# A fused decoder layer on one core: ten weight-pair sums moved from the up projection into attention, and five pairs by seven products in four chunks

## The chip, the cores and the metric

The kernel runs on one core of one Trainium2 chip. Its time is the device time of one execution, in microseconds (us). The profile is one further execution with the hardware profiler on; its spans and instruction times are those of that execution.

## The reference

One decoder layer on 256 positions of width 2048, all in float32:

```
p = rmsnorm(x) @ w_in                      # q, k, v of 8 heads; latents of 8 more
A = dilated window attention(q, k, v); B = latent attention
x = x + rmsnorm(concat(A, B) @ w_out)
h = rmsnorm(x) * gain
u = square(relu(h @ w_up))                 # w_up: 2048 x 8192
out = x + rmsnorm(u @ w_down)              # w_down: 8192 x 2048
```

## The kernel before

**Precision and tiles.** Each float32 operand is split into a rounded part `hi` and a rest `lo`; a product takes three matmuls (hi hi, hi lo, lo hi), each 128x128 by 128x512. ScalarE makes `hi` (L293, or L297 with a gain folded in), VectorE `lo` (L294, L298). `Weights` streams weight tiles of 128 x 1024 in the order in which they were planned: a load into one of 5 `raw` buffers on the SP queue, then the split into one of 8 `hi`/`lo` buffers. When TensorE's program begins tile i, the splits up to tile i+6 have been issued. Every engine takes its instructions strictly in the order issued. `Flow` writes that order down: a clock advanced by estimated matmul times, and chains (generators) that issue their next piece when the clock reaches it.

**Stages.** Projections and both attentions to about 300 us, the output projection to about 350, the up projection to about 700, the down projection to the end. The two halves of x stand in `xs` from the start; they are used for the first norm (`prelude`, `pre`), then not until `powers` scales them by `pw` during the output projection (L829).

**The up projection.** Eight chunks (j = 0 to 7) of 1024 columns. In chunk 0, 16 tiles of 128 rows (steps "k") go by 12 matmuls each (2 token blocks x 2 halves x 3). In chunks 1 to 7 three pairs of tiles (rows 0 to 5, steps "w" 0, 1, 2) go by seven products instead of eight: 21 matmuls per pair instead of 24. That needs sums of the four quarter blocks of a pair on the weights' side, called t and u, and sums of h on the other side (`left_sums`). The order of a chunk is k6 to k10, w0, k11, k12, w1, k13, w2, k14, k15. For a "w" step POOL loads the two raw tiles into the buffer `ab` (L360; there is one, so the next pair waits until the last split of the earlier one has read it), VectorE makes t and u (L345, L349, L350: "pair sums"), and four tiles are split from SBUF: a quarter (512 wide), b, u and t (1024 wide each). The sums are issued two tiles ahead of the pair's first tile. A "k" tile has the norm's gain folded into its split.

`left_sums(kp)` adds hi and lo of h for one pair, scales by the gain, makes the sums (L963 to L973), and puts the scaled h back in place. The seven products also use four extra accumulators m[1], m[6], m[7], m[5], in the banks of the previous chunk; after the last pair `close` combines them into `c`: a copy on ScalarE (L1005) and four VectorE operations (L1008):

```
scalar.activation(c[0], m[1], AF.Copy)
for out, x, y, op in ((1, m[6], c[0], SUB), (2, m[7], c[1], SUB),
                      (1, m[5], c[1], ADD), (3, c[1], m[7], SUB)):
    tt(out=c[out], in0=x, in1=y, op=op)
```

The next chunk accumulates in those four banks, in the order m[1], m[6], m[7], m[5]. Meanwhile `up_evac` empties the last chunk's four accumulators, one after another: VectorE adds `c` (L909), ScalarE makes `r` (relu, L912), TensorE transposes it (`rt`, L287), ScalarE squares (L924).

Of the kernel before, what the change touches and what calls it, by code (L numbers as in the profile page):

```python
# [92 lines left out]
D_UP, UP_STEP = 1.8, 2.2  # L93


N_SEVEN, SUMS_AHEAD = 3, 2
UP_STEPS = [("k", k) for k in range(6, 11)]
for _i, _n in enumerate(((11, 12), (13,), (14, 15))):
    UP_STEPS += [("w", _i)] + [("k", k) for k in _n]


DOWN_SEVEN = ((7, 11, 13, 17, 19, 23, 25, 29), (4, 7, *range(9, 28, 2)))
# [148 lines left out]
def layer(nc, tc, io):  # L251
# [77 lines left out]
        return io["w_up"][k * P:(k + 1) * P, j * CW:(j + 1) * CW]  # L329

    late = {}

    def seven(load, targets):

        st, tt, H = {}, nc.vector.tensor_tensor, 512

        def sums():
            ab = load()  # L340
            a, b = st["a"], st["b"] = [ab[:, :CW], ab[:, CW:]] if not isinstance(ab, list) else ab
            t, u = st["t"], st["u"] = targets()
            if not isinstance(ab, list):
                two = [x.rearrange("p (k n) -> p k n", n=H) for x in (t, ab)]
                tt(out=two[0], in0=two[1][:, 0:2, :], in1=two[1][:, 1:4:2, :], op=OP.add)  # L345
            else:
                for x, o in ((a, 0), (b, H)):
                    tt(out=t[:, o:o + H], in0=a[:, o:o + H], in1=x[:, H:], op=OP.add)
# [14 lines left out]
    def seven_up(j, kp):  # L363
        def load():
            if j == FF // CW - 1 and kp:
                return [weights.load(up_weight(j, 2 * kp + i), CW, f"raw_w{j}_{kp}{i}") for i in range(2)]
            return load_two(late["ab"], nc.gpsimd if (j, kp) > (1, 0) else nc.sync,
                            io["w_up"][2 * kp * P:(2 * kp + 2) * P, j * CW:(j + 1) * CW])
# [30 lines left out]


    wide_u, after = [], 0
    for j in range(FF // CW):
        wide_u.append([])
        for what, k in [("k", k) for k in range(KD)] if j == 0 else UP_STEPS:
            if what == "k":
                ts = [weights.plan(up_weight(j, k), 1, CW, gcol[:, 8 + k:9 + k])]
            else:
                ts, after = plan_seven(*seven_up(j, k), after)
            wide_u[j].append((what, k, ts))
# [121 lines left out]
    def prelude():  # L531
# [14 lines left out]
        nc.vector.reduce_sum(ss0, ss0h, axis=mybir.AxisListType.X)  # L546
        rstd0.append(rstd_of(ss0, NB, D, "pre"))

    def tables():

        yield D_TAB[0]
        nc.scalar.dma_start(out=pos_i, in_=io["pos"])
        nc.scalar.dma_start(out=cst, in_=io["consts"])
        yield D_TAB[1]
        pos_f = con.tile([P, NB], F32, name="pos_f")
        nc.vector.tensor_copy(pos_f, pos_i)
        ang = pa.tile([P, 2, NB, 96], F32, tag="qkT", bufs=2, name="ang")
# [12 lines left out]
        yield 4.0  # L570
        nc.scalar.activation(trig, ang, AF.Sin)
# [77 lines left out]

    pre = flow.start(prelude())  # L650
    tab = flow.start(tables())
    heads, evacs = [], []
    for half in range(2):
        qkv = {}
# [156 lines left out]
    def powers():  # L811
        po, g_post = late["po"], late["g_post"]
        yield 8.0
        for n in range(4):
            junk = po.tile([P, 512], BF16, tag="junk", bufs=1, name=f"junkg{n}")
            nc.scalar.activation(junk, g_post[:, n * 512:(n + 1) * 512], AF.Square, accum_out=gg4[:, n:n + 1])
            yield 1.5
        nc.vector.reduce_sum(gg, gg4, axis=mybir.AxisListType.X)
        nc.vector.tensor_scalar_add(pws[:, 3, :], ss0, gg)
        r = rstd_of(pws[:, 3, :], NB, D, "pw")  # L820
        yield 2.0
        nc.vector.tensor_single_scalar(out=pw.bitcast(I32), in_=r.bitcast(I32), scalar=0x7F800000, op=OP.bitwise_and)
        nc.vector.tensor_single_scalar(out=pwi.bitcast(I32), in_=pw.bitcast(I32), scalar=0x7F800000, op=OP.bitwise_xor)
        nc.vector.tensor_scalar_mul(pwi, pwi, 0.5)
        for i, (v, c) in enumerate(((pwi, 1.0 / D), (pwi, EPS), (pw, EPS))):
            nc.vector.scalar_tensor_tensor(out=pws[:, i, :], in0=v, scalar=c, in1=v, op0=OP.mult, op1=OP.mult)
        for b in range(NB):
            for c in (slice(0, CW), slice(CW, D)):
                nc.vector.tensor_scalar_mul(xs[b][:, c], xs[b][:, c], pw[:, b:b + 1])  # L829
                yield 1.5  # L830
# [74 lines left out]
    def up_evac(j, b, i, acc, order, more=None):  # L905
# [11 lines left out]
        if j not in uT:  # L917
            if j in (12, 13):
                t2 = late["ab"][:, (j - 12) * CW:(j - 11) * CW]
            else:  # L920
                tag = {"tag": "T", "bufs": 2} if j > 13 else {}
                t2 = late["up"].tile([P, CW], F32, name=f"uT{j}", **tag)
# [35 lines left out]
    def left_sums(kp):  # L958
# [5 lines left out]
        for i in range(2):  # L964
            nc.vector.tensor_scalar_mul(f[:, i * S:(i + 1) * S], f[:, i * S:(i + 1) * S], gcol[:, 8 + k + i:9 + k + i])
        four_sums(q, f)
        st = [late["st"][:, i * 512:(i + 1) * 512] for i in (2 * kp, 2 * kp + 1)]
        yield 3.0
        for t, x in ((hs, f), (st, q)):
            nc.scalar.activation(t[0], x, AF.Copy)  # L970
# [3 lines left out]
        sums.append([[t[:, i * P:(i + 1) * P] for t in st] for i in range(4)])  # L974
        yield 0.5

    def all_sums():
        for kp in range(N_SEVEN - 1):
            yield from left_sums(kp)
        yield 8.0  # L980
        yield from left_sums(N_SEVEN - 1)

    def three(out, a, w, first, last):

# [3 lines left out]
    def seven_products(ts, left, accs, m, first, last):  # L988
# [2 lines left out]
        prods = ((a11, 0, 0, 1), (a12, 1, 0, (0, 0)), (s4, 1, 1, (0, 1)), (s2, 2, 0, 6), (a22, 2, 1, (1, 0)),  # L991
                 (s3, 3, 1, 7), (s1, 3, 0, 5))
        for p, (a, i, half, to) in enumerate(prods):
            w = weights.get(ts[i])
            in_m = isinstance(to, int)
            three(m[to] if in_m else accs[to], a, [w[x][:, half * 512:half * 512 + 512] for x in range(2)],
                  in_m and first, in_m and last)
# [18 lines left out]
    for j in range(FF // CW):  # L1016
# [9 lines left out]
        for t, b in order:  # L1026
            what, k, tiles = steps[t]
            if (j, t, b) == (0, 8, 0):
# [4 lines left out]
                late["st"] = late["up"].tile([P, 3 * CW], F32R, tag="st", bufs=1, name="st")  # L1033
                for n in ("ab", "c"):
                    late[n] = late["up"].tile([P, 2 * CW], F32, name=n)
                flow.start(all_sums())
            if (j, t, b) == (FF // CW - 1, 4, 0):
                weights.limit -= 1
                u_next = split_u(0, 0)
            if j == 1 and what == "w":  # L1040
                flow.until(lambda: len(sums) > k)
            if what == "k":
                w = weights.get(tiles[0])
# [220 lines left out]
```

## Time and profile before

| | us |
|---|---|
| median of 3 runs (1052.40 to 1053.32) | 1052.87 |
| the profiled execution, its own time | 1052.05 |
| its span, first to last instruction | 1050.3 |
| TensorE (PE) busy | 1039.0 |
| VectorE (DVE) busy | 811.0 |
| ScalarE (ACT) busy | 625.4 |
| POOL busy | 61.5 |

The span leaves out 1.75 us of the execution's own time. Rows of a timeline give start, duration, engine, line, operation, output <- inputs, shape and count; a bracket at the end is the idle time before it and what ended it. Rows of the stage table give the stretch, its length, the busy time of PE, PEld, DVE, ACT and POOL, the granted clock (1.00 is full), the DMA engines' share and GB/s. A wait row gives total, count and longest.

### The profile page before, as it was taken

The numbers are of one execution on the slowest core, as the hardware profiler recorded it, in microseconds if no ns is written. First come the engines' busy times: TensorE is split into PE (matmuls) and PEld (weight loads), VectorE is DVE, ScalarE is ACT, GpSimd is POOL, SyncE is SP. The second block draws the span as 40 slices with busy tenths as digits, with TensorE's granted clock in tenths as the row PEclk, the third lists the DMA queues.
The fourth block names the chain that finished last, engine by engine and source line by source line (L and its number), as shares of the span: only waits on it lengthen the run. The fifth ranks groups of instructions, "written<-read, shape, count | busy, mean of one in ns | idle before, by whom it ended". The sixth has DMA issues, their size and how long they took to land.

```text
span 1050.3 us, 13459 instructions
## 1 busy us (share of the span) xinstructions
PE 1039.0 (99%) x4854; PEld 865.9 (82%) x4854; DVE 811.0 (77%) x1080; ACT 625.4 (60%) x834; POOL 61.5 (6%) x116
## 2 busy tenths in 40 slices
PE   9999999999999999999999999999999999999996
PEld 6888899888888788888888888888888888888885
DVE  6676536577557679879888798887899978989995
ACT  6675436565555467666665666666567564766661
POOL 0000000000000000010000000000000001112100
PEclk9999999999999999999999999999999999999999
DMA  8975447454447295646556465469788767788952
GB/s 298 371 230 155 140 127 239 141 166 155 141 170 234 77 344 174 224 143 238 194 189 201 145 234 194 151 227 319 246 276 315 267 223 259 268 300 313 381 186 81
DMA packets 80643, 229.34 MB, mean 218 GB/s; under 512 B 7616, under 2 KB 12224, under 8 KB 80192
## 3 DMA queue, kind: packets, MB, share of 16 engines
q1 hardware_dynamic: 65888, 176.45, 50.3%
q0 software_dynamic: 14112, 51.39, 14.2%
q8 instruction: 38, 0.62, 0.2%
q10 hardware_dynamic: 576, 0.64, 0.2%
q14 instruction: 29, 0.24, 0.1%
HBM read 212.72 MB, written 15.73 MB: 218 GB/s over the span
## 4 chain that ended last, share of the span: by engine, by line
PE 96%; DVE 1%; DMA 1%; issue 1%; ACT 0%; POOL 0%; DVEq 0%; POOLq 0%; ACTq 0%
PE y L283 26%; PE acc_u L283 26%; PE acc_o L283 8%; PE m L283 5%; PE md L283 5%; PE acc_v L283 4%; PE acc_qk L283 4%; PE acc_ckv L283 2%; PE acc_ukv L283 2%; PE acc_q L283 2%; PE acc_cq L283 2%; PE acc_k L283 2%; PE acc_uq L283 2%; PE rt L287 1%; PE sc_b L283 1%
## 5 line engine op out<-in xcount | busy, mean ns | idle before, releaser
L294 DVE TENSOR_TENSOR lo<-raw,hi 128x1024 fp32r<-128x1024 f32 (+3 forms) x213 | 241.7, 1152 | 91.5 <-ACT hi L293 90.7
L293 ACT ACTIVATE hi<-raw 128x1024 fp32r<-128x1024 f32 (+3 forms) x213 | 209.5, 999 | 77.6 <-PE y L283 20.8
L283 PE MATMUL acc_u<-hi,hT_hi 128*128 128x512 f32 x386 | 153.3, 397 | 0.0
L283 PE MATMUL acc_u<-hi,hT_lo 128*128 128x512 f32 x386 | 151.0, 391 | 0.4 <-DVE hT_lo L294 0.4
L283 PE MATMUL acc_u<-lo,hT_hi 128*128 128x512 f32 x386 | 150.7, 391 | 0.0
L283 PE MATMUL y<-hi,uhi 128*128 128x512 f32 x376 | 146.8, 390 | 0.0
L283 PE MATMUL y<-hi,ulo 128*128 128x512 f32 x376 | 146.5, 390 | 0.0
L283 PE MATMUL y<-lo,uhi 128*128 128x512 f32 x376 | 146.5, 390 | 0.0
L298 DVE SCALAR_TENSOR_TENSOR lo<-raw,gcol,hi 128x1024 fp32r<-128x1024 f32 x86 | 107.6, 1280 | 11.2 <-ACT hi L297 11.0
L297 ACT ACTIVATE hi<-raw,gcol 128x1024 fp32r<-128x1024 f32 x86 | 97.8, 1151 | 24.8 <-PE acc_u L283 10.9
L283 PEld LDWEIGHTS acc_u<-hi,hT_lo 128*128 128x128 f32 x386 | 72.5, 188 | 16.1 <-DVE hT_lo L294 0.8
L283 PEld LDWEIGHTS acc_u<-lo,hT_hi 128*128 128x128 f32 x386 | 72.6, 188 | 14.2
L283 PEld LDWEIGHTS acc_u<-hi,hT_hi 128*128 128x128 f32 x386 | 72.6, 188 | 13.9
L283 PEld LDWEIGHTS y<-hi,uhi 128*128 128x128 f32 x376 | 70.6, 188 | 14.6
L283 PEld LDWEIGHTS y<-hi,ulo 128*128 128x128 f32 x376 | 70.6, 188 | 14.6
L283 PEld LDWEIGHTS y<-lo,uhi 128*128 128x128 f32 x376 | 70.6, 188 | 14.5
L283 PE MATMUL acc_o<-hi,mixT_hi 128*128 128x512 f32 x128 | 51.9, 405 | 0.0
L294 DVE TENSOR_TENSOR lo<-st_down,hi 128x1024 fp32r<-128x1024 f32 x40 | 48.1, 1220 | 4.0 <-ACT hi L293 3.8
L283 PE MATMUL acc_o<-hi,mixT_lo 128*128 128x512 f32 x128 | 50.2, 392 | 0.0
L283 PE MATMUL acc_o<-lo,mixT_hi 128*128 128x512 f32 x128 | 50.0, 391 | 0.0
L293 ACT ACTIVATE hi<-ab 128x512 fp32r<-128x512 f32 (+1 forms) x38 | 32.0, 842 | 29.3 <-PE acc_u L283 24.4
L293 ACT ACTIVATE hi<-st_down 128x1024 fp32r<-128x1024 f32 x40 | 42.1, 1053 | 11.1 <-PE y L283 9.5
(322 smaller groups left out, 1986.3 us busy)
## 6 DMA issues: line engine op xcount, KB each, us to landing
raw<-in_w_down SPq DMA_DIRECT2D x88, 512.0 KB, 6.0
raw<-in_w_up SPq DMA_DIRECT2D x86, 512.0 KB, 4.5
raw<-in_w_in SPq DMA_DIRECT2D x55, 512.0 KB, 5.0
ab<-in_w_up POOLq DMA_DIRECT2D x36, 512.0 KB, 5.0
raw<-in_w_out SPq DMA_DIRECT2D x32, 512.0 KB, 4.3
ab_down<-in_w_down POOLq DMA_DIRECT2D x20, 512.0 KB, 6.4
ukeep<-ulo SPq DMA_DIRECT2D x15, 512.0 KB, 7.2
ulo<-ukeep POOLq DMA_DIRECT2D x15, 512.0 KB, 5.4
```

The source lines that it names most:

```text
L283: nc.tensor.matmul(out, a, b, start=start, stop=stop)
L287: nc.tensor.transpose(out, a, ident)
L293: nc.scalar.activation(hi, src, AF.Copy)
L294: nc.vector.tensor_tensor(out=lo, in0=src, in1=hi.bitcast(F32), op=OP.subtract)
L297: nc.scalar.activation(hi, src, AF.Copy, scale=g)
L298: nc.vector.scalar_tensor_tensor(out=lo, in0=src, scalar=g, in1=hi.bitcast(F32), op0=OP.mult, op1=OP.subtract)
```

## The change

For ten pairs of w_up (pairs 0 and 2 of chunk 1, pairs 3 and 4 of chunks 2 to 5) the sums t and u are made during attention. A chain `prepare` uses x's two buffers, which are idle after the first norm: POOL loads the raw pair into one, VectorE makes t and u in the other 16 us of the flow's clock later, POOL writes them to HBM (`sums_kept`); after the tenth, x is loaded again, and `powers` waits for that chain and 8 us more. In the up projection a prepared pair (step "p") comes as four loads on the SP queue through `raw`: the quarter and b from w_up, u and t from `sums_kept`. Chunks 2 to 5 then do five pairs by seven products (0 to 4; k10 to k15 remain), in the order k10 k11 k12 w0 p3 w1 k13 w2 p4 k14 k15. Chunk 1 does pairs 0 and 2 prepared, 1 as before. Chunks 6 and 7 keep three pairs. `left_sums` runs for pairs 3 and 4 in chunk 1; since it leaves h scaled, k6 to k9 of chunks 6 and 7 are split without the gain. The sums of h for pairs 3 and 4 stand in a buffer that chunk 5's output uses afterwards.

```diff
@@ -93,10 +93,24 @@
 D_UP, UP_STEP = 1.8, 2.2
-N_SEVEN, SUMS_AHEAD = 3, 2
-UP_STEPS = [("k", k) for k in range(6, 11)]
-for _i, _n in enumerate(((11, 12), (13,), (14, 15))):
-    UP_STEPS += [("w", _i)] + [("k", k) for k in _n]
+SUMS_AHEAD = 2
+NUP = FF // CW
+def steps_of(text):
+    return [(s[0], int(s[1:])) for s in text.split()]
+UP_STEPS = {0: [("k", k) for k in range(KD)]}
+UP_STEPS[1] = steps_of("k6 k7 k8 k9 k10 p0 k11 k12 w1 k13 p2 k14 k15")
+for _j in range(2, 6):
+    UP_STEPS[_j] = steps_of("k10 k11 k12 w0 p3 w1 k13 w2 p4 k14 k15")
+for _j in range(6, NUP):
+    UP_STEPS[_j] = steps_of("k6 k7 k8 k9 k10 w0 k11 k12 w1 k13 w2 k14 k15")
+SCALED = {1: range(6), **{j: range(10) for j in range(2, NUP)}}
+PREP = [(j, k) for j in UP_STEPS for w, k in UP_STEPS[j] if w == "p"]
+D_PREP = (16.0, 1.5, 1.0, 1.0)
 DOWN_SEVEN = ((7, 11, 13, 17, 19, 23, 25, 29), (4, 7, *range(9, 28, 2)))
@@ -329,6 +343,18 @@
         return io["w_up"][k * P:(k + 1) * P, j * CW:(j + 1) * CW]
     late = {}
+    sums_kept = {jk: dram.tile([P, 2 * CW], F32, name=f"sums{jk[0]}_{jk[1]}") for jk in PREP}
+    def pair_sums(ab, t, u):
+        H, tt = 512, nc.vector.tensor_tensor
+        two = [x.rearrange("p (k n) -> p k n", n=H) for x in (t, ab)]
+        tt(out=two[0], in0=two[1][:, 0:2, :], in1=two[1][:, 1:4:2, :], op=OP.add)
+        yield D_PREP[1]
+        tt(out=u[:, :H], in0=t[:, :H], in1=ab[:, 3 * H:], op=OP.add)
+        yield D_PREP[2]
+        tt(out=u[:, H:], in0=u[:, :H], in1=ab[:, 2 * H:3 * H], op=OP.add)
+        yield D_PREP[3]
     def seven(load, targets):
@@ -399,11 +424,17 @@
     wide_u, after = [], 0
-    for j in range(FF // CW):
+    for j in range(NUP):
         wide_u.append([])
-        for what, k in [("k", k) for k in range(KD)] if j == 0 else UP_STEPS:
+        for what, k in UP_STEPS[j]:
             if what == "k":
-                ts = [weights.plan(up_weight(j, k), 1, CW, gcol[:, 8 + k:9 + k])]
+                g = () if k in SCALED.get(j, ()) else (gcol[:, 8 + k:9 + k],)
+                ts = [weights.plan(up_weight(j, k), 1, CW, *g)]
+            elif what == "p":
+                kept = sums_kept[j, k]
+                ts = [weights.plan(src, 1, n) for src, n in (
+                    (up_weight(j, 2 * k)[:, :512], 512), (up_weight(j, 2 * k + 1), CW),
+                    (kept[:, CW:], CW), (kept[:, :CW], CW))]
             else:
                 ts, after = plan_seven(*seven_up(j, k), after)
             wide_u[j].append((what, k, ts))
@@ -546,6 +577,20 @@
         nc.vector.reduce_sum(ss0, ss0h, axis=mybir.AxisListType.X)
         rstd0.append(rstd_of(ss0, NB, D, "pre"))
+    def prepare():
+        ab, tu = xs
+        while pre in flow.chains:
+            yield 0.5
+        for j, kp in PREP:
+            load_two(ab, nc.gpsimd, io["w_up"][2 * kp * P:(2 * kp + 2) * P, j * CW:(j + 1) * CW])
+            yield D_PREP[0]
+            yield from pair_sums(ab, tu[:, :CW], tu[:, CW:])
+            nc.gpsimd.dma_start(out=sums_kept[j, kp], in_=tu)
+        yield 2.0
+        for b in range(NB):
+            nc.gpsimd.dma_start(out=xs[b], in_=io["x"][b * P:(b + 1) * P, :])
     def tables():
         yield D_TAB[0]
@@ -649,6 +694,7 @@
     pre = flow.start(prelude())
     tab = flow.start(tables())
+    prep = flow.start(prepare())
     heads, evacs = [], []
     for half in range(2):
         qkv = {}
@@ -824,6 +870,9 @@
         nc.vector.tensor_scalar_mul(pwi, pwi, 0.5)
         for i, (v, c) in enumerate(((pwi, 1.0 / D), (pwi, EPS), (pw, EPS))):
             nc.vector.scalar_tensor_tensor(out=pws[:, i, :], in0=v, scalar=c, in1=v, op0=OP.mult, op1=OP.mult)
+        while prep in flow.chains:
+            yield 0.5
+        yield 8.0
         for b in range(NB):
             for c in (slice(0, CW), slice(CW, D)):
                 nc.vector.tensor_scalar_mul(xs[b][:, c], xs[b][:, c], pw[:, b:b + 1])
@@ -964,7 +1017,8 @@
         for i in range(2):
             nc.vector.tensor_scalar_mul(f[:, i * S:(i + 1) * S], f[:, i * S:(i + 1) * S], gcol[:, 8 + k + i:9 + k + i])
         four_sums(q, f)
-        st = [late["st"][:, i * 512:(i + 1) * 512] for i in (2 * kp, 2 * kp + 1)]
+        sp, i0 = (late["st"], 2 * kp) if kp < 3 else (late["st2"], 2 * kp - 6)
+        st = [sp[:, i * 512:(i + 1) * 512] for i in (i0, i0 + 1)]
         yield 3.0
         for t, x in ((hs, f), (st, q)):
             nc.scalar.activation(t[0], x, AF.Copy)
@@ -974,11 +1028,10 @@
         sums.append([[t[:, i * P:(i + 1) * P] for t in st] for i in range(4)])
         yield 0.5
-    def all_sums():
-        for kp in range(N_SEVEN - 1):
+    def some_sums(kps, after=0.0):
+        yield after
+        for kp in kps:
             yield from left_sums(kp)
-        yield 8.0
-        yield from left_sums(N_SEVEN - 1)
     def three(out, a, w, first, last):
@@ -991,7 +1044,7 @@
         prods = ((a11, 0, 0, 1), (a12, 1, 0, (0, 0)), (s4, 1, 1, (0, 1)), (s2, 2, 0, 6), (a22, 2, 1, (1, 0)),
                  (s3, 3, 1, 7), (s1, 3, 0, 5))
         for p, (a, i, half, to) in enumerate(prods):
-            w = weights.get(ts[i])
+            w = [x[:, 0, :] if len(x.shape) == 3 else x for x in weights.get(ts[i])]
             in_m = isinstance(to, int)
             three(m[to] if in_m else accs[to], a, [w[x][:, half * 512:half * 512 + 512] for x in range(2)],
                   in_m and first, in_m and last)
@@ -1033,11 +1086,15 @@
                 late["st"] = late["up"].tile([P, 3 * CW], F32R, tag="st", bufs=1, name="st")
                 for n in ("ab", "c"):
                     late[n] = late["up"].tile([P, 2 * CW], F32, name=n)
-                flow.start(all_sums())
+                late["st2"] = late["up"].tile([P, 2 * CW], F32R, tag="uT10", bufs=1, name="st2")
+                flow.start(some_sums((0, 1)))
+                flow.start(some_sums((2,), 18.0))
+            if (j, t, b) == (1, 4, 0):
+                flow.start(some_sums((3, 4), 6.0))
             if (j, t, b) == (FF // CW - 1, 4, 0):
                 weights.limit -= 1
                 u_next = split_u(0, 0)
-            if j == 1 and what == "w":
+            if what != "k":
                 flow.until(lambda: len(sums) > k)
             if what == "k":
                 w = weights.get(tiles[0])
@@ -1052,7 +1109,8 @@
                     weights.free(tiles[0])
                 continue
-            first, last = k == 0, k == N_SEVEN - 1
+            pairs = [s[1] for s in steps if s[0] != "k"]
+            first, last = k == pairs[0], k == pairs[-1]
             if first:
                 m = {n: bank(i, f"m{n}_{j}") for n, i in zip((1, 6, 7, 5), free)}
             blocks = [[tok(hT[x], 2 * k + kk, bb) for x in range(2)] for kk, bb in ((0, 0), (1, 0), (1, 1))]
...
```

More of the change, by code (lines that the diff above doesn't have):

```diff
@@ L343, in sums @@
             if not isinstance(ab, list):
[L344 to L348, printed above, removed]
+                for _ in pair_sums(ab, t, u):
+                    pass
+                return
+            for x, o in ((a, 0), (b, H)):
+                tt(out=t[:, o:o + H], in0=a[:, o:o + H], in1=x[:, H:], op=OP.add)
             tt(out=u[:, :H], in0=t[:, :H], in1=b[:, H:], op=OP.add)
@@ L366, in load @@
                 return [weights.load(up_weight(j, 2 * kp + i), CW, f"raw_w{j}_{kp}{i}") for i in range(2)]
-            return load_two(late["ab"], nc.gpsimd if (j, kp) > (1, 0) else nc.sync,
-                            io["w_up"][2 * kp * P:(2 * kp + 2) * P, j * CW:(j + 1) * CW])
+            return load_two(late["ab"], nc.gpsimd, io["w_up"][2 * kp * P:(2 * kp + 2) * P, j * CW:(j + 1) * CW])
         return seven(load, lambda: [late["up"].tile([P, CW], F32, tag="T", bufs=2, name=f"{n}{j}_{kp}") for n in "tu"])
@@ L919, in up_evac @@
                 t2 = late["ab"][:, (j - 12) * CW:(j - 11) * CW]
+            elif j in (10, 11):
+                if j == 10:
+                    late["uT10"] = late["up"].tile([P, 2 * CW], F32, tag="uT10", bufs=1, name="uT10")
+                t2 = late["uT10"][:, (j - 10) * CW:(j - 9) * CW]
             else:
```

## The prediction, made before the changed kernel ran

> **What bounds the kernel now.** I read the page's busy table first, then the chain that ended last, then TensorE's and VectorE's waits in the up stage, then the timelines of one up chunk.
>
> ```profile
> span 1050.3 us, 13459 instructions
> PE 1039.0 (99%) x4854; PEld 865.9 (82%) x4854; DVE 811.0 (77%) x1080; ACT 625.4 (60%) x834; POOL 61.5 (6%) x116
> ...
> 493.74 0.44 PE rt L287 x4
> 526.25 10.88 PE acc_u L283 x48
> 537.14 0.44 PE rt L287 x4
> ...
> PE acc_u L283 <- DVE hT_lo L294: 0.4, 1, 0.4
> ```
>
> TensorE works 99% of the span, and its waits between 300 and 720 us (last row) come to 0.4 us. A matmul takes 10.88 / 48 = 0.2267 us. Chunks repeat every 43.40 us (493.74 to 537.14). Of the 48 matmuls at 526.25 the first 24 are k14 and k15, so the next chunk starts at 526.25 + 5.44 = 531.69. As long as TensorE never waits, a matmul removed is time removed. So the question is whether VectorE, the next engine, stays ahead in the chunks that change.
>
> ```profile
> 490.80:534.20 43.40, 43.40 (x200) 35.94 (x200) 37.07 (x40) 27.16 (x31) 3.22 (x7) 1.00 0.59 194
> 760.00:850.00 90.00, 90.00 (x399) 74.56 (x398) 82.84 (x94) 56.99 (x61) 5.38 (x10) 1.00 0.84 292
> ...
> DVE t L345 <- DMA ab<-in_w_up: 12.0, 5, 2.9
> ```
>
> The third busy time of a stage row is VectorE's: 37.07 us of a 43.40 us chunk. The wait row (447 to 664 us, five chunks) names a part of its idle time that does not depend on TensorE: 12.0 / 5 = 2.4 us a chunk for the raw pair `ab`. This is one chunk on VectorE:
>
> ```profile
> 493.07 1.29 DVE L909 TENSOR_TENSOR acc_u<-acc_u,c 128x512 f32<-128x512 f32 x2
> 495.95 1.23 DVE L294 TENSOR_TENSOR lo<-t,hi 128x1024 fp32r<-128x1024 f32 x1 [1.59 <-ACT hi L293]
> 497.10 0.69 DVE L909 TENSOR_TENSOR acc_u<-acc_u,c 128x512 f32<-128x512 f32 x1
> 497.70 1.22 DVE L345 TENSOR_TENSOR t<-ab 128x1024 f32<-128x1024 f32 x1
> 500.28 2.48 DVE L298 SCALAR_TENSOR_TENSOR lo<-raw,gcol,hi 128x1024 fp32r<-128x1024 f32 x2
> 504.94 1.23 DVE L294 TENSOR_TENSOR lo<-ab,hi 128x1024 fp32r<-128x1024 f32 x1 [1.32 <-ACT hi L293]
> 506.08 1.22 DVE L294 TENSOR_TENSOR lo<-u,hi 128x1024 fp32r<-128x1024 f32 x1
> 507.22 1.22 DVE L294 TENSOR_TENSOR lo<-t,hi 128x1024 fp32r<-128x1024 f32 x1
> 510.50 1.23 DVE L345 TENSOR_TENSOR t<-ab 128x1024 f32<-128x1024 f32 x1 [2.06 <-DMA ab<-in_w_up]
> 513.10 1.28 DVE L298 SCALAR_TENSOR_TENSOR lo<-raw,gcol,hi 128x1024 fp32r<-128x1024 f32 x1
> 514.30 1.82 DVE L294 TENSOR_TENSOR lo<-ab,hi 128x512 fp32r<-128x512 f32 x2
> 518.30 3.67 DVE L298 SCALAR_TENSOR_TENSOR lo<-raw,gcol,hi 128x1024 fp32r<-128x1024 f32 x3
> 527.70 1.28 DVE L298 SCALAR_TENSOR_TENSOR lo<-raw,gcol,hi 128x1024 fp32r<-128x1024 f32 x1
> 528.90 2.27 DVE L1008 TENSOR_TENSOR c<-m,c 128x512 f32<-128x512 f32 x3
> 531.21 0.69 DVE L1008 TENSOR_TENSOR c<-c,m 128x512 f32<-128x512 f32 x1
> 531.81 1.28 DVE L298 SCALAR_TENSOR_TENSOR lo<-raw,gcol,hi 128x1024 fp32r<-128x1024 f32 x1
> ```
>
> Prices from start to start: a 1024-wide `lo` 1.14 (506.08 to 507.22), a scaled one 1.20 (527.70 to 528.90), pair sums 2.58 (497.70 to 500.28), the four splits of a pair 4.00 (514.30 to 518.30), an evacuating add 0.60 (497.10 to 497.70), `close` 2.91 (528.90 to 531.81). The tightest spot: `close`'s last subtraction reads m[7], whose bank the next chunk writes six matmuls (1.36 us) after its start, at 533.05. It ended at 531.81 + about 0.09: some 1.2 us of slack in every chunk.
>
> **The change, part by part.**
>
> *Matmuls.* Chunks 2 to 5 turn two more pairs from 24 to 21 matmuls: 4 x 2 x 3 x 0.2267 = 5.44 us less on TensorE, 1.36 a chunk (42.04 instead of 43.40). Chunks 1, 6 and 7 keep their counts.
>
> *VectorE in chunks 2 to 5.* Four scaled splits go (4 x 1.20 = 4.8), two prepared pairs come (2 x 4.00): 37.07 + 3.2 = 40.3 us of work. With the 2.4 us wait for `ab` that is 42.7 us, already over TensorE's 42.04. In order on VectorE, from the end of one `close` to the next:
>
> First part, with the evacuation in it. Three splits of w0 (3.42), add 0 (0.60), the 512-wide split of p3 (0.59), then add 1 starts at 4.6. What follows add 1 is a round trip:
>
> ```profile
> 493.80 0.69 ACT L912 ACTIVATE r<-acc_u,rstd_pre 128x512 f32<-128x512 f32 x1 [1.04 <-DVE acc_u L909]
> 494.39 0.59 ACT L924 ACTIVATE uT<-rt 128x512 f32<-128x512 f32 x1
> 494.86 1.06 ACT L293 ACTIVATE hi<-t 128x1024 fp32r<-128x1024 f32 x1
> ```
>
> ScalarE takes r (493.80), the square behind the first transposes (494.39), and only then the next `hi` (494.86), so the `lo` behind it ends at 497.10, 4.03 us after add 1 began. The new order puts the second tile of p3 in that place: 4.6 + 4.0 = 8.6. Then add 3 (0.60), w1's sums (2.58), two splits of p3 (2.28), w1's first two splits (1.82): w1's `ab` is free at 15.9. w2's sums can only start when its pair has landed:
>
> ```profile
> 506.46 0.54 POOL L360 DMA_DIRECT2D ab<-in_w_up  x1 [2.01 <-DVE lo L294]
> raw<-in_w_up SPq DMA_DIRECT2D x11, 512.0 KB, 3.8
> ab<-in_w_up POOLq DMA_DIRECT2D x7, 512.0 KB, 5.0
> 514.40 6.73 SPq L175 DMA_DIRECT2D raw<-in_w_up  x3
> DMA to landing us min/median/max: 3.5/3.8/4.8
> ```
>
> The split that freed it ended at 506.17, sums began at 510.50: 4.33 us, and with the stage's mean wait (2.4 instead of 2.06) 4.67. w1, k13, w2 keep their order, so this wait stays. First part: 15.9 + 4.7 = 20.6 us.
>
> Second part: sums 2.59, k13 1.20, w2 4.00, p4 4.00, k14 1.20, k15 and k10 2.40, w0's sums 2.59, k11 and k12 2.40, w0's 512-wide split 0.60, `close` 2.91: 23.9 us. To this a new wait: prepared pairs take four of the five `raw` buffers, so k15's load goes out only when p4's first split is done (the queue issues at 514.40, just as the split begun at 513.10 ends). Landing 4.3 (between the median 3.8 and the longest 4.8, as w0's pair and k14 load alongside), `hi` 1.15 and 0.1 make 5.6 us, against VectorE work of 3 x 1.14 + 1.20 = 4.6: a wait of 1.0. Second part 24.9; the whole loop 45.5 us, 3.5 over TensorE's 42.04.
>
> *Chunk by chunk.* Chunk 2 begins on time: its transposes stand at 5.44, the `lo` behind them ends 3.36 later (493.74 to 497.10) at 8.8; + 0.6 + 2.58 + 2.28 + 1.82 + 4.67 = 20.8; + 24.9 = 45.7, needed at 42.04 + 1.36 = 43.40: TensorE waits 2.3. Chunks 3 and 4 add 3.5 each. Chunk 5 adds 3.8, since what then stands ahead of `close` is 4 x 1.14 instead of 4.2. Together 13.1 us of new waits.
>
> *Chunk 1.* The sums of pairs 0 and 2 leave (2 x 2.58) with the wait ahead of pair 2, and two left sums arrive:
>
> ```profile
> 404.04 0.68 DVE L963 TENSOR_TENSOR c<-hT_hi,hT_lo 128x512 f32<-128x512 f32 x1
> 406.40 1.22 DVE L294 TENSOR_TENSOR lo<-ab,hi 128x1024 fp32r<-128x1024 f32 x1
> ...
> 62.95 0.71 POOL L485 TENSOR_TENSOR rstd_pre<-t_pre,neg_half 128x2 f32<-128x2 f32 x1 [61.61 <-DVE t_pre L484]
> 322.06 0.75 DVE L829 TENSOR_SCALAR x<-x,pw 128x1024 f32<-128x1024 f32 x1
> ```
>
> Each is 2.36 (404.04 to 406.40) + two 512-wide splits of 0.6 = 3.6. The balance is within 1.5 us, `close` has 1.2 of slack: taken as 0, bound 0 to 1.8. Chunks 6 and 7 do four cheaper splits each: nothing.
>
> *Preparation.* The rows above and these:
>
> ```profile
> 50.00:124.00 74.00, 74.00 (x350) 61.63 (x349) 47.41 (x89) 44.77 (x71) 0.71 (x1) 1.00 0.63 190
> ...
> PE qrt L287 <- DVE qT L744: 0.2, 1, 0.2
> ```
>
> Ten pair sums, 26 us of VectorE in pieces of at most 1.22, from 63 us (the norm's last step on POOL) at about 21 us apiece to about 280; x comes back before it is scaled at 322, which moves some 8 us later and is still ahead of the residual. The loads have 16 us, landing takes 5; POOL issues 32 more transfers of 0.54 between three small powers. VectorE works 47.4 of 74 us from 50 to 124 and TensorE's one wait on it in attention is 0.2 us, so I count nothing on the path; if every piece delayed a softmax step a little, 0 to 2 us.
>
> Sum: -5.4 + 13.1 = +7.7; 1052.05 (the profiled execution's own time) + 7.7 = 1059.8. The runs' median is 0.8 above that execution, so I say 1060.
>
> *A rule on transfers.* The rows: pairs land in 5.0 us at a DMA share of 0.59; in the down stage, at 0.84, in 6.4.
>
> ```profile
> ab_down<-in_w_down POOLq DMA_DIRECT2D x20, 512.0 KB, 6.4
> ```
>
> A changed chunk moves 9.96 MB instead of 8.39, in 42 us a share of about 0.72, so halfway: +0.7 us on each `ab` landing, 2.8 us over four chunks, and up to as much again on k15's load. That gives 1063 to 1066, the upper end. The Trainium skill, "DMA: Bandwidth & Descriptors", "Issuing engines are not separate DMA queues", states that transfers run on the same 16 DMA engines whichever engine issues them; by that the new loads on SP slow POOL's pairs, as an estimate to that upper end, and the two rows agree with it in direction. I keep the rows of the up stage for the sum, because no chunk of before has this mix.
>
> **Rivals.** *VectorE keeps up* (the other side). The lead is real: w2's last split ends at 518.30, TensorE first reads it six matmuls before 526.25, at 524.9, and nothing waits now. If pairs landed behind other VectorE work and k15's load came in time, 2.4 + 1.0 us a chunk would go and the loop would be at TensorE's 42: the whole 5.4 us, 1047.4. It decides from a loop under about 42.3. Against it: 40.3 us of pure work leave 1.7 for a wait that now takes 2.4.
>
> *VectorE is the bound but only just.* The evacuation's round trip costs 8.6 - 6.4 = 2.2 us of the loop; if ScalarE's order let p3's tile through, and k15's load landed in 3.5, the loop would be 42.6 to 43.4: 1049 to 1054.
>
> *Preparation disturbs attention*, alone or besides: ten pieces of 1.22 us wholly on TensorE's path would be 12 us, 1059 to 1064 with the gain kept. For it: softmax chains run across VectorE in order. Against: TensorE's waits there are 0.2 us, and VectorE is a third idle.
>
> **How the numbers follow.** About 0.2% (2.1 us) is what a measurement of this kernel tells from no change. VectorE's loop decides: 0.61, time 1055 to 1067 (both loads at their shortest: 4 x 0.34 + 4 x 0.8 less, 1055; with the crowded DMA and 1 to 2 us from chunk 1 or preparation, 1067). Just bound: 0.15. Keeps up: 0.19. Preparation alone: 0.05. Slower: 0.61 + 0.05 and a little of the second, 0.67; faster: 0.19 and a little of the second, 0.21; same 0.12. The range, 1047.4 to 1065, takes in the gain's edge and leaves out the last of the contention; the likeliest case alone is 1055 to 1067.
>
> **What would show it.** Right: TensorE waits in chunks 3 to 6 for `close`'s subtractions (`acc_u` behind VectorE's `c`) or for the first transposes, 2 to 4 us per chunk; chunk periods of 44 to 46; VectorE over 90% busy there, waiting about 2 us for `ab`, and ScalarE waiting for `raw` at k15. Wrong: periods of 42.0 and no TensorE wait (first rival); waits of TensorE before 300 us (third). My least certain step is the order in which ScalarE's squares and `hi` stand, and the landing times under a load that the trace doesn't hold.

## Result and profile after

The changed kernel takes 1080.8 us (1080.06 to 1082.14, 4 runs) against 1053.1 for the kernel before on the same chip: ratio 1.0265, 95% interval 1.0247 to 1.0283, 27.7 us slower. The forecast was 1060.0 with a range of 1047.4 to 1065: slower, and by the mechanism named, but 20 us too little.

The page of the changed kernel, its span, busy times and the chain that ended last by engine:

```profile
span 1077.9 us, 13631 instructions
...
PE 1044.7 (97%) x4830; PEld 863.8 (80%) x4830; DVE 848.0 (79%) x1136; ACT 633.9 (59%) x854; POOL 76.5 (7%) x146
...
PE 79%; DVE 11%; DMA 4%; issue 3%; ACT 2%; DVEq 0%; POOL 0%; POOLq 0%; ACTq 0%
```

The chain of the kernel before:

```profile
PE 96%; DVE 1%; DMA 1%; issue 1%; ACT 0%; POOL 0%; DVEq 0%; POOLq 0%; ACTq 0%
```

TensorE has its 24 matmuls less (4854 to 4830), but 21% of the chain is no longer TensorE's, where it was 4%. Where the 27.6 us of span came in is read from a few marks on TensorE: the first product of `acc_v`, and the first transposes (`rt`) of each chunk. Kernel before:

```profile
49.66 0.39 PE L283 MATMUL acc_v<-hi,xT_hi 128*128 128x512 f32 x1
...
403.38 0.60 PE L287 MATMUL rt<-ident,r 128*128 128x128 f32 x4
450.18 0.60 PE L287 MATMUL rt<-ident,r 128*128 128x128 f32 x4
623.77 0.60 PE L287 MATMUL rt<-ident,r 128*128 128x128 f32 x4
```

The changed kernel, chunks 1 to 6:

```profile
51.16 0.39 PE L297 MATMUL acc_v<-hi,xT_hi 128*128 128x512 f32 x1
...
411.21 0.60 PE L301 MATMUL rt<-ident,r 128*128 128x128 f32 x4
458.70 0.66 PE L301 MATMUL rt<-ident,r 128*128 128x128 f32 x4 [0.36 <-ACT r L961]
507.22 0.66 PE L301 MATMUL rt<-ident,r 128*128 128x128 f32 x4 [0.36 <-ACT r L961]
555.19 0.66 PE L301 MATMUL rt<-ident,r 128*128 128x128 f32 x4 [0.34 <-ACT r L961]
603.14 0.66 PE L301 MATMUL rt<-ident,r 128*128 128x128 f32 x4 [0.35 <-ACT r L961]
651.77 0.66 PE L301 MATMUL rt<-ident,r 128*128 128x128 f32 x4
```

- Start: 1.5 us (51.16 against 49.66), ahead of anything that the change touches. In the runs below this mark lies between 49.0 and 51.2, so about a microsecond either way in one profile means nothing.
- Attention and the rest up to chunk 1: 360.05 instead of 353.72, 6.3 us.
- Chunks 1 to 5: 240.56 instead of 220.39, 20.2 us; with the 5.44 us of matmuls that went, 25.6 us of new time. The four changed chunks last 48.52, 47.97, 47.95 and 48.63 us instead of 43.40. Behind them 0.4 us come back.

What TensorE waits for there (changed kernel, 404 to 660 us; total, count, longest):

```profile
PE acc_u L297 <- DVE c L1061: 9.7, 7, 2.0
PE acc_u L297 <- DVE lo L312: 7.5, 4, 2.0
PE rt L301 <- ACT r L961: 1.4, 4, 0.4
```

One changed chunk by engines (stage table of the changed kernel):

```profile
543.00:591.00 48.00, 43.30 (x194) 34.30 (x193) 40.26 (x44) 28.63 (x36) 3.17 (x6) 1.00 0.63 207
```

Waits for `close` (`c`) and for the first transposes were foretold; waits for a split just ahead of a tile (`lo`) were not. VectorE's work is 40.26 us, as worked out (40.3). The other 7.7 us of the loop it stands idle, and its timeline in chunk 3 says where:

```profile
502.35 1.22 DVE L308 TENSOR_TENSOR lo<-ab,hi 128x1024 fp32r<-128x1024 f32 x1
...
506.95 1.29 DVE L958 TENSOR_TENSOR acc_u<-acc_u,c 128x512 f32<-128x512 f32 x2
509.84 1.23 DVE L308 TENSOR_TENSOR lo<-raw,hi 128x1024 fp32r<-128x1024 f32 x1 [1.59 <-ACT hi L307]
...
516.44 1.86 DVE L308 TENSOR_TENSOR lo<-ab,hi 128x512 fp32r<-128x512 f32 x2
...
524.56 1.23 DVE L352 TENSOR_TENSOR t<-ab 128x1024 f32<-128x1024 f32 x1 [4.00 <-DMA ab<-in_w_up]
...
538.70 1.29 DVE L312 SCALAR_TENSOR_TENSOR lo<-raw,gcol,hi 128x1024 fp32r<-128x1024 f32 x1 [1.05 <-ACT hi L311]
540.62 1.28 DVE L312 SCALAR_TENSOR_TENSOR lo<-raw,gcol,hi 128x1024 fp32r<-128x1024 f32 x1 [0.63 <-ACT hi L311]
...
550.32 1.22 DVE L308 TENSOR_TENSOR lo<-ab,hi 128x1024 fp32r<-128x1024 f32 x1
```

From 502.35 to 550.32 one loop takes 47.97 us, with three stalls: 1.59 us behind an evacuating add (ScalarE's relu and square stand ahead of the `hi`), 4.00 for w2's pair, 1.05 and 0.63 for k15 and k10, whose loads come late.

In attention TensorE waits twice, 1.6 us for `kr` and 2.3 us for a `qT` copy:

```profile
PE qrt L301 <- DVE qT L790: 2.3, 1, 2.3
PE krt L301 <- DVE kr L630: 1.6, 1, 1.6
```

VectorE ahead of that copy:

```profile
259.92 1.22 DVE L352 TENSOR_TENSOR x<-x 128x1024 f32<-128x1024 f32 x1
...
262.92 0.69 DVE L354 TENSOR_TENSOR x<-x,x 128x512 f32<-128x512 f32 x1
...
264.65 0.68 DVE L356 TENSOR_TENSOR x<-x,x 128x512 f32<-128x512 f32 x1
265.26 0.68 DVE L790 COPY qT<-qt 128x512 f32<-128x512 f32 x1
```

All three pieces of one prepared pair (2.6 us) stand ahead of the copy that TensorE needs. Two pieces of another pair stand ahead of `kr`, at 214.80 and 216.54 us. The two waits are 3.9 of the 6.3 us; 1.6 more are slow matmuls behind the second (last section), and the remaining 0.8 is not traced.

### The profile page after: what moved, and what is told of

Read it like the earlier page. It is cut to its first block, busy times and chain, and to the rows that moved or that the text cites. A ratio compares the mean times of both kernels' runs of the same rounds, so it can differ in the third digit from the quotient of the medians.

```text
span 1077.9 us, 13631 instructions
## 1 busy us (share of the span) xinstructions
PE 1044.7 (97%) x4830; PEld 863.8 (80%) x4830; DVE 848.0 (79%) x1136; ACT 633.9 (59%) x854; POOL 76.5 (7%) x146
## 4 chain that ended last, share of the span: by engine, by line
PE 79%; DVE 11%; DMA 4%; issue 3%; ACT 2%; DVEq 0%; POOL 0%; POOLq 0%; ACTq 0%
PE y L297 25%; PE acc_u L297 14%; PE acc_o L297 8%; PE md L297 5%; DVE lo L308 4%; PE acc_qk L297 4%; PE acc_v L297 4%; PE m L297 3%; PE acc_ckv L297 2%; DMA ab<-in_w_up 2%; PE acc_q L297 2%; PE acc_cq L297 2%; PE acc_k L297 2%; DVE lo L312 2%; DMA raw<-in_w_up 1%
## 5 line engine op out<-in xcount | busy, mean ns | idle before, releaser
L308 DVE TENSOR_TENSOR lo<-raw,hi 128x1024 fp32r<-128x1024 f32 (+3 forms) x261 | 293.5, 1143 | 89.4 <-ACT hi L307 88.6
L307 ACT ACTIVATE hi<-raw 128x1024 fp32r<-128x1024 f32 (+3 forms) x261 | 254.0, 992 | 83.8 <-PE y L297 20.0
L297 PE MATMUL acc_u<-hi,hT_hi 128*128 128x512 f32 x338 | 135.5, 401 | 9.7 <-DVE c L1061 9.7
L297 PE MATMUL acc_u<-lo,hT_hi 128*128 128x512 f32 x338 | 132.8, 393 | 7.5 <-DVE lo L312 7.5
L297 PE MATMUL acc_u<-hi,hT_lo 128*128 128x512 f32 x338 | 132.9, 393 | 0.5 <-DVE hT_lo L308 0.5
L312 DVE SCALAR_TENSOR_TENSOR lo<-raw,gcol,hi 128x1024 fp32r<-128x1024 f32 x62 | 78.5, 1280 | 15.0 <-ACT hi L311 14.9
L311 ACT ACTIVATE hi<-raw,gcol 128x1024 fp32r<-128x1024 f32 x62 | 70.6, 1148 | 32.3 <-DMA raw<-in_w_up 18.1
L297 PEld LDWEIGHTS acc_u<-hi,hT_hi 128*128 128x128 f32 x338 | 63.8, 189 | 25.2 <-DVE c L1061 13.2
L297 PEld LDWEIGHTS acc_u<-hi,hT_lo 128*128 128x128 f32 x338 | 63.8, 189 | 14.5 <-DVE hT_lo L308 0.9
L297 PE MATMUL m<-hi,st 128*128 128x512 f32 x174 | 64.4, 394 | 0.0
L307 ACT ACTIVATE hi<-st_down 128x1024 fp32r<-128x1024 f32 x40 | 42.1, 1052 | 11.3 <-PE y L297 9.5
```

The source lines that it names most:

```text
L297: nc.tensor.matmul(out, a, b, start=start, stop=stop)
L307: nc.scalar.activation(hi, src, AF.Copy)
L308: nc.vector.tensor_tensor(out=lo, in0=src, in1=hi.bitcast(F32), op=OP.subtract)
L311: nc.scalar.activation(hi, src, AF.Copy, scale=g)
L312: nc.vector.scalar_tensor_tensor(out=lo, in0=src, scalar=g, in1=hi.bitcast(F32), op0=OP.mult, op1=OP.subtract)
```

## The experiments

My theory: VectorE's loop, made of in-order work and three stalls, sets the time of the changed chunks, and the preparation costs something only where its pieces stand ahead of what TensorE needs next. Rivals: the preparation costs by its amount of work or transfers wherever it stands; reading the sums back from HBM slows the up stage; the stalls come from the DMA engines being shared, so that order hardly helps.

**1. The preparation alone.** The ten pairs are prepared as in the change, the up projection is the old one.

```diff
-UP_STEPS[1] = steps_of("k6 k7 k8 k9 k10 p0 k11 k12 w1 k13 p2 k14 k15")
-    UP_STEPS[_j] = steps_of("k10 k11 k12 w0 p3 w1 k13 w2 p4 k14 k15")
+UP_STEPS[1] = steps_of("k6 k7 k8 k9 k10 w0 k11 k12 w1 k13 w2 k14 k15")
+    UP_STEPS[_j] = steps_of("k6 k7 k8 k9 k10 w0 k11 k12 w1 k13 w2 k14 k15")
...
```

> Left out: nothing of the computation; the ten sums are made and written during attention as in the change, but the up projection is that of the kernel before and never reads them. Theory (two costs that add): attention loses what the trace of the changed kernel shows ahead of 270 us and the up projection nothing, so 1059 to 1061 (before 1053 + 6 to 8), with TensorE waiting for VectorE at krt and qrt. Rival (preparation costs nothing by itself, the up projection carries all 28 us): 1053. Rival (preparation carries most): above 1065.

1059.03 us, ratio 1.0059 (1.0044 to 1.0075): this version costs 5.9 us. The waits of 1.6 and 2.3 us are there again, and from `acc_v` to chunk 1's transposes its profile takes 6.3 us more than before, as in the changed kernel. A further 1.6 us are in chunk 1 (48.41 us instead of 46.80, 1.4 of it a wait for the first relu), where a left sum stands a little later than before; its start is 0.6 us earlier and its end 0.5 shorter. So the attention's part is read from the marks, not from the total.

**2. The up projection alone.** No preparation: the two tiles of sums are read from other rows of w_up, so the output is not the layer's.

```diff
-    prep = flow.start(prepare())
-                    (kept[:, CW:], CW), (kept[:, :CW], CW))]
+                    (up_weight(j, 2 * k), CW), (up_weight(j, 2 * k + 1), CW))]
...
```

> Left out: the preparation; sums t and u are loaded from other rows of w_up instead, so bytes, queues and the order of the up projection are those of the change, and the numbers are not the layer's. Theory: the up projection alone costs 20 to 21 us, so 1073 to 1074, with the same loop of 48.0 us per chunk. Rival (what costs is reading back from freshly written HBM): the loop falls towards 45 and the time to 1062 or less.

1074.23 us, ratio 1.0205 (1.0188 to 1.0222): 21.1 us, and with the 5.9 of the first run 27.0 of the 27.7. Its loops are 47.2, 48.4, 49.5 and 49.0 us, no shorter than the changed kernel's. So what slows the up stage is neither the work in attention nor that the sums were just written to HBM.

**3. p4 ahead of w2.** Only the order of chunks 2 to 5 changes.

```diff
-steps_of("k10 k11 k12 w0 p3 w1 k13 w2 p4 k14 k15")
+steps_of("k10 k11 k12 w0 p3 w1 p4 k13 w2 k14 k15")
```

> The changed kernel with p4 and k13 exchanged in chunks 2 to 5: k10 k11 k12 w0 p3 w1 p4 k13 w2 k14 k15. Same instructions, same transfers. Theory (VectorE's order around two loads): w2's pair now lands behind p4's four splits, and four tiles of w2 that need no raw buffer stand between p4 and k14, so the waits for ab (4.0 to 4.4) and for raw (1.8) go: loop 48.0 to 42.0 to 42.6, 21 to 23 us less, 1058 to 1060. Rival (VectorE or the DMA engines are bound by amount, not by order): still 46 to 48 a chunk, 1076 to 1081.

1059.63 us, ratio 1.0061 (1.0046 to 1.0076): 21 us given back by an order. VectorE's waits, 460 to 640 us, first the changed kernel, then this one:

```profile
DVE t L352 <- DMA ab<-in_w_up: 17.0, 4, 4.4
DVE lo L312 <- ACT hi L311: 6.7, 7, 1.7
DVE lo L308 <- ACT hi L307: 6.6, 5, 1.6
```

```profile
DVE lo L308 <- ACT hi L307: 8.0, 5, 1.6
DVE t L352 <- DMA ab<-in_w_up: 4.9, 6, 1.6
```

p4's four splits now cover the landing of w2's pair, and k15's load no longer stands behind them: the waits for `raw` are gone, those for `ab` fall by 12 us. The landing itself is no shorter (median 5.4 us here, 5.5 in the changed kernel, between 490 and 574 us). The round trip's 1.59 us a loop stays, and the loop is 43.2 to 43.6 us, not the 42.0 to 42.6 that I had expected: just the pace of before.

**4. A second buffer for w2's pair** in chunks 2 to 4 (the place of two later output tiles).

```diff
-            return load_two(late["ab"], ...
+            return load_two(late["spare" if kp == 2 and 2 <= j < 5 else "ab"], ...
...
```

> The changed kernel, but in chunks 2, 3 and 4 w2's raw pair goes to a second buffer (the place of two later output tiles), so that its load need not wait for w1's splits. Theory: the ab wait of 4.0 to 4.4 goes in three chunks and nothing takes its place but the raw wait of 1.8, which stays: loop 44 there, 12 us less, 1069. Rival (DMA engines crowded): the wait moves to raw and less than 6 us is gained.

1063.74 us, ratio 1.0108 (1.0091 to 1.0126), 17 us less where 12 were expected. In the profiles the stretch from chunk 1's to chunk 6's transposes is 14.0 us shorter; the rest stands ahead of chunk 1, whose mark comes 3.0 us earlier here (1.35 of it the start, 1.65 attention), which the edit does not touch. The wait for `ab` is gone in these chunks, and the loops are 43.4, 44.2 and 42.9 us; the waits at k15 and for the round trip stay.

**5. Two places for p4's tiles** in chunks 2 to 4, so that k15's load need not wait for p4's first split.

```diff
+                if k == 4 and j < 5:
+                    for i in range(2):
+                        weights.place[ts[i]] = lambda i=i: late["spare"][:, i * CW:(i + 1) * CW]
...
```

> The changed kernel, except that in chunks 2, 3 and 4 the first two tiles of p4 land in two places of their own, so k15's load no longer waits for p4's first split. My theory: the two waits of VectorE there for a split whose load came late, 1.05 + 0.63 us and about 1.85 with what surrounds them, go in three loops; TensorE's waits shrink by 3 x 1.85 = 5.5 us: 1074 to 1077 us, loop 46.1 us. Rival (the loads share the DMA engines, and what comes earlier in one place comes later in another): the wait for w2's pair grows by as much, 1079 to 1081 us.

1073.08 us, ratio 1.0197 (1.0182 to 1.0213); the loops are 45.81, 45.83 and 45.97 us (46.1 expected). This stall is worth 2.1 us a loop, and what it gives is not taken back elsewhere; the time is a microsecond under what I expected, and the marks ahead of chunk 1 come 2.6 us earlier in this profile.

**6. The preparation earlier:** 9 instead of 16 of the flow's clock between a load and its sums, up stage as before.

```diff
-D_PREP = (16.0, 1.5, 1.0, 1.0)
+D_PREP = (9.0, 1.5, 1.0, 1.0)
...
```

> The preparation alone (up stage as before), with 9 instead of 16 between a pair's load and its sums, so the ten pairs are done by about 210 us instead of 290. Theory (the place decides: only pieces that stand ahead of the k and q steps after 212 us are on TensorE's path): the waits of 1.6 (krt) and 2.3 (qrt) and the slow matmuls behind them go, 1053 to 1055 us. Rival (26 us of VectorE's work costs its 6 us wherever it is put, or the sums now wait for their loads): 1058 to 1060 us.

1061.92 us, ratio 1.0090 (1.0076 to 1.0103): worse than the 1059.0 of the old spacing. As expected the two waits went (0.2 us for `qT` is left), but new ones came, and attention takes 8.5 us more than before. TensorE's longest wait from 40 to 400 us:

```profile
PE acc_cq L297 <- ACT ckv L741: 3.7, 1, 3.7
```

ScalarE's timeline ahead of it, and then the landing times between 160 and 185 us:

```profile
176.39 1.06 ACT L307 ACTIVATE hi<-raw 128x1024 fp32r<-128x1024 f32 x1 [3.84 <-DMA raw<-in_w_in]
```

```profile
raw<-in_w_in SPq DMA_DIRECT2D x7, 512.0 KB, 9.5
```

Pairs 15 us apart, on top of the stage with the densest weight loads, make those loads land in 9.5 us. In the same window they took 4.7 us in the kernel before, 5.8 with pairs 21 us apart (run 1). ScalarE, in order, stands behind one of them, and TensorE behind ScalarE. So there are two prices: pieces ahead of a needed step, and transfers where the loads are dense. My theory had only the first.

**7. p4 ahead of w2, and seven tiles ahead instead of six** in chunks 2 to 5, which puts ScalarE's `hi` of p3's second tile ahead of the first relu.

```diff
+            if (t, b) == (0, 0) and j in (2, 6):
+                weights.ahead = 7 if j == 2 else W_AHEAD
...
```

> Order with p4 ahead of w2, and in chunks 2 to 5 VectorE and ScalarE prepare seven tiles ahead instead of six, which puts ScalarE's hi of p3's second tile ahead of the first relu, and VectorE's sums of w1 between the evacuating adds. Theory (the loop of 43.2 to 43.6 us still holds 1.6 us of wait for that hi, which is the round trip): the loop falls to TensorE's 42.04, and four chunks give 5 us: 1053.5 to 1056 us against 1059.6 with six ahead. Rival (the waits for ab take its place, since the pair is asked for no earlier): the loop stays at 43, 1058 to 1060 us.

1055.89 us (1053.38 to 1057.40), ratio 1.0026 (1.0017 to 1.0036). VectorE's loop: its first evacuating adds come at 454.86, 496.98, 539.49, 581.58 and 623.16 us, 42.1 us apart on the mean. The round trip was the last stall of that size, and with it gone VectorE's loop is at TensorE's 42.04. TensorE's own marks in these chunks lie 42.3 to 42.5 us apart.

**8. Both edits, 6 and 7.**

> The two last edits together. Theory: nothing of the preparation on the path and the loop at TensorE's pace: the whole 5.4 us of the 24 matmuls, 1047.5 to 1050 us. If only the early preparation works: 1053 to 1055; if only the seven tiles ahead work: 1053 to 1056; if neither: 1058 to 1060 us.

1058.79 us, ratio 1.0053 (1.0041 to 1.0066), not the 1047.5 to 1050 that I had expected: the early preparation costs 3 us more than the old one, as alone. The number falls where neither edit was to work, but TensorE's marks in the changed chunks are 42.3 to 42.5 us apart, as in run 7.

**9. Half the bytes** for the three wide tiles of each prepared pair, in the changed kernel's order; the second half of their columns is not the reference's.

```diff
+                half = i in self.half
+                if half:
+                    src, w = src[:, :512], 512
...
+                self.split_fn(two[0], two[1], raw[:, :512].unsqueeze(1).to_broadcast([P, 2, 512]), g)
...
```

> The changed kernel, with the three wide tiles of each prepared pair in chunks 2 to 5 loaded at half their bytes (the split reads the 512 loaded columns twice, so their second half is not the reference's): 1.5 MB less in a chunk, the same instructions on every engine. If the long landing of w2's pair (6.26 us from the split that frees it to its sums, against 4.33 before) and the late k15 come from transfers that share the DMA engines: the first falls to 4.3 to 5.3 and the waits at k15 by 0.5 or more, the loop from 48.0 to 46 to 47 us, 1074 to 1077 us. If the landing is long for another reason (the issue on POOL, the order of the two halves): loop 48, 1079 to 1082 us.

1077.50 us, ratio 1.0232 (1.0211 to 1.0254), between the two expectations. VectorE's waits, 460 to 640 us:

```profile
DVE t L362 <- DMA ab<-in_w_up: 12.0, 4, 3.2
...
DVE lo L322 <- ACT hi L321: 6.5, 6, 2.0
```

The wait for the pair falls from 17.0 to 12.0 us, 1.25 a chunk, and from the freeing split to the sums it is 5.2 instead of 6.3 us: shared transfers are that part of the long landing. The waits for `raw` do not fall (6.5 against 6.7): k15's load is late because its buffer comes free late, as run 5 shows, and not for the bytes of the tiles ahead of it.

What the bytes are worth in time, this run does not tell. VectorE's loops are 46.9, 47.2, 48.8 and 47.5 us, but TensorE's stretch from chunk 1 to chunk 6 is only 0.6 us shorter than the changed kernel's (239.93 against 240.56); the other 2.5 us of the profile lie ahead of it. At the start of the third loop the granted clock had fallen (0.93 in this row, where the changed kernel's row above had 1.00), TensorE's transposes came late, and the wait of the round trip was 3.41 us instead of 1.59:

```profile
508.00:556.00 48.00, 44.57 (x189) 35.40 (x188) 39.21 (x43) 27.82 (x34) 3.18 (x6) 0.93 0.55 175
```

```profile
554.67 1.23 DVE L318 TENSOR_TENSOR lo<-raw,hi 128x1024 fp32r<-128x1024 f32 x1 [3.41 <-ACT hi L317]
```

**10. As 7, without the preparation** (what the up stage gives by itself; the sums are again other rows of w_up).

> Order with p4 ahead of w2 and seven tiles ahead, but no preparation in attention (the two tiles of sums are read from other rows of w_up, so the output is not the reference's). This is what the up stage's products are worth by themselves once VectorE keeps up: my theory says the whole 5.4 us, 1047 to 1049 us. Rival (reading 41 instead of 33 tiles in a chunk still costs something): 1050 to 1053 us.

1049.88 us, ratio 0.9968 (0.9956 to 0.9981): 3.2 us faster, not 5.4. That lies between my range and the rival's.

**11 and 12. As 7, with the preparation placed** around the k steps (213 us) and the q step (259 us).

```diff
-D_PREP = (16.0, 1.5, 1.0, 1.0)
+D_PREP = ((*[14.5] * 7, 26.0, 25.0, 10.0), 1.5, 1.0, 1.0)
...
-            yield D_PREP[0]
+            yield D_PREP[0][n]
...
```

In run 12 the ten delays are 16 six times, then 31, 10, 16 and 10.

> p4 ahead of w2, seven tiles ahead, and the preparation placed: the first seven pairs 19.5 us apart instead of 21, so the seventh is done before the k steps at 213 us; the eighth at about 236; the ninth behind the q step of 259 us. Theory (only pieces ahead of those two steps are on TensorE's path): waits of 1.6 and 2.3 us and the slow matmuls behind the second gone, 1049 to 1052 us. Rival (every pair costs a little by its transfers, wherever it stands; pairs closer together make the weight loads of 160 to 180 us late, as at 14 us apart): 1054 to 1058 us.

> As the run before, with another placement: the first six pairs at the old spacing, the seventh put behind the k and q steps, at about 229 us, the eighth at 245, the ninth behind the q step of 259 us, the tenth at about 283. Theory: 1049 to 1052 us, with no weight load late at 160 to 180 us. Rival: 1054 to 1058 us.

1051.35 us, ratio 0.9982 (0.9973 to 0.9991), and 1049.68 us, ratio 0.9971 (0.9962 to 0.9981). The last is as fast as the run without any preparation, and the fastest version with the whole work in it: 3.1 us under the kernel before. TensorE's longest wait in it from 30 to 1000 us:

```profile
PE rt L301 <- ACT r L961: 1.0, 1, 1.0
```

Its marks on TensorE:

```profile
50.85 0.39 PE L297 MATMUL acc_v<-hi,xT_hi 128*128 128x512 f32 x1
...
404.58 0.60 PE L301 MATMUL rt<-ident,r 128*128 128x128 f32 x4
452.66 0.66 PE L301 MATMUL rt<-ident,r 128*128 128x128 f32 x4 [0.97 <-ACT r L961]
...
622.94 0.60 PE L301 MATMUL rt<-ident,r 128*128 128x128 f32 x4
```

From `acc_v` to chunk 1's transposes it takes 353.73 us, to a hundredth what it took before (353.72): the same 26 us of VectorE and the same transfers cost nothing where no one waits behind them. So the rival that they cost by their amount falls. Chunks 1 to 5 take 218.36 us against 220.39. Of the 5.44 us, 1.3 go in chunk 1 to 2 (48.08 instead of 46.80; 0.97 is the wait for the first relu, and run 10 has the same 48.07 without any preparation). The four chunks last 42.57 us each on average, 0.5 over 42.04. What takes it is probably the waits of TensorE's weight loads, 440 to 630 us, where the kernel before has none:

```profile
PEld rt L301 <- ACT r L961: 2.1, 4, 1.4
PEld m L297 <- ACT uT L977: 1.7, 4, 0.4
PEld acc_u L297 <- DVE c L1061: 1.6, 4, 0.6
```

With a pair so early in the chunk, an accumulator `m` meets a bank that still holds transposes for ScalarE's square (the second row). No run takes these waits away, so that they make up the 0.5 us is not shown.

## Why the prediction failed

Of the span, 19.9 us were missed: 12.5 in chunks 1 to 5 (25.6 us of new time instead of 13.1), 6.3 in attention (counted as 0) and 1.5 in the start, less the 0.4 behind chunk 5. That VectorE's in-order loop would set the pace of the changed chunks was right. The steps that failed are the times of two loads in that loop, and the preparation put at nothing.

*Matmuls, -5.44.* Right in number. In time only about 2 of it could be had in the profile of run 12, for the waits just shown. I had counted no cost for the earlier place of the first pair.

*VectorE's work and order, 40.3 us.* Right to the tenth (40.26), and so is the table: w1's first two splits end 15.95 us into the loop (502.35 to 518.30) against 15.9, the split behind the round trip ends at 8.6.

*The landing of w2's pair, 4.67.* Mis-sized: 6.26 (518.30 to 524.56), and 6.4 to 6.7 in the other three chunks. I took the stage's mean of before, although the text itself held the reason to expect more, and put that into the upper end at 0.7 us. It was 1.6 in this loop; with half the prepared pairs' bytes the same stretch took 5.2 (run 9). The DMA share by which I scaled was wrong too: 0.72 in the forecast, 0.63 here, since the loop was longer; but from 518 to 521 us, just after the pair was asked for, it was 0.96. The mean does not tell how crowded the transfers are at that moment. The Trainium skill, "DMA: Bandwidth & Descriptors", "Issuing engines are not separate DMA queues", says that transfers interleave on the same engines whoever issued them; runs 6 and 9 agree, and the sum by it would have been the nearer one, though still 15 to 18 us short.

*k15's load, a wait of 1.0.* Named rightly, mis-sized: 1.85 (1.05 and 0.63 and what lies between), 2.1 by run 5. The loop is thus 47.97 instead of 45.5: 1.6 and 0.85 more.

*Chunk by chunk, 13.1.* The first changed chunk was to lose 2.3, because it begins on time; it lost 6.5 (48.52 against 42.04). It did begin on time: its transposes stood 0.36 us late. But the split behind them was done 9.6 us into the chunk (462.45; the chunk began at 452.90, which is 5.44 and the 0.36 ahead of the transposes at 458.70) instead of 8.8, the pair's landing took 6.7 instead of 4.67, and k15 cost 2.0 instead of 1.0: some 3.8 of the 4.2 us missing. Chunks 3 to 5 lost 5.9, 5.9 and 6.6 against 3.5, 3.5 and 3.8; chunk 1 lost 0.7 (bound 0 to 1.8). Sum 25.6. Of the signs I gave, the waits for `c` and the first transposes, for `ab` and at k15 came (TensorE's waits were larger than foretold, 18.6 us in four chunks), and so did waits before 300 us, the sign of the third rival; periods of 44 to 46 and a VectorE busy over 90% did not: it was busy for 84% (40.26 of 48), since the longer loop is all waiting, and even the forecast's own 40.3 of 45.5 is only 89%.

*Preparation, 0 with a bound of 2.* The step that failed in kind. I counted that VectorE is a third idle and that TensorE's waits there were 0.2 us; but that very row, `qrt` behind `qT`, said that this place had no slack at all. One pair's pieces fell on it, two of another's on `kr`, and attention took 6.3 us more (here and in run 1), and 0.0 more when they were placed elsewhere (run 12). The third rival had it, at 0.05 for the case alone.

*The rivals.* "VectorE keeps up" and "just bound" fall for this order; the first came true for the loop of another (run 7), the second nearly (run 3, loops of 42.9 to 43.6). The range left out the joint of two cases: a slower loop and a disturbed attention.

## What to carry to other kernels

Idle time of an engine is no cover by itself: look for the rows in which TensorE waits on it for even 0.2 us, and keep inserted work away from those places. For an in-order engine add up one whole loop, with each load's time from the instruction that frees the buffer to the one that needs it, and ask for each wait what other work could stand there: here one swap in the order gave 21 us, though the best version is only 3.1 us under the kernel before. Take a landing time from the most crowded moment, not from the stage's mean.

## What the runs showed of the hardware

The same wait of 2.31 us ahead of `qrt` had two prices. In the changed kernel the matmuls behind it ran at about half pace for 3 us. The stage table of that stretch (granted clock 0.66), and TensorE's timeline:

```profile
265.00:270.00 5.00, 4.00 (x13) 3.31 (x14) 3.54 (x8) 0.38 (x1) 1.60 (x3) 0.66 0.83 272
```

```profile
266.00 0.56 PE L301 MATMUL qrt<-ident,qr 128*128 128x128 f32 x2 [2.31 <-DVE qT L790]
...
266.78 0.63 PE L297 MATMUL acc_o<-lo,mixT_hi 128*128 128x512 f32 x1
...
269.92 0.49 PE L301 MATMUL pT_b<-ident,s_b 128*128 128x128 f32 x3
```

In run 7, after the same wait, they did not:

```profile
264.69 0.44 PE L301 MATMUL qrt<-ident,qr 128*128 128x128 f32 x2 [2.31 <-DVE qT L790]
...
265.20 0.39 PE L297 MATMUL acc_o<-lo,mixT_hi 128*128 128x512 f32 x1
...
267.00 0.49 PE L301 MATMUL pT_b<-ident,s_b 128*128 128x128 f32 x3
```

From `qrt` to `pT_b` it is 3.92 us in the one and 2.31 in the other: 1.6 us that one execution pays and another doesn't. In run 9 it was two shorter waits for `c`: 1.49 and 1.35 us, with 1.0 us of matmuls between, were followed by 5.7 us of matmuls 0.43 us apart (545.50 to 551.21), the drop seen above. In the changed kernel 1.22 and 1.35 us, just as close (ending at 548.14 and 550.46), were followed by matmuls 0.23 us apart.

The Trainium skill, "TensorE: Matmul & The Clock Gate", "Part 1: The HAM clock gate", says that the clock is halved after an idle window of about 3.4 us, in windows that run freely. The rows agree that it depends on the moment; that 2.3 us can be enough is not in that sentence.
